# Four accumulators with sums in place, fewer late chunks, and the residual's bias moved within DRAM, in a two-layer backbone on TensorE

## The chip, the cores and the metric

The kernel runs on one core of one Trainium2 chip. The metric is device time in microseconds (us) of one execution. The engines are TensorE (PE in the profile, with its weight loads as PEld), VectorE (DVE), ScalarE (ACT), GpSimd (POOL) and SyncE (SP). Data lies in DRAM, in the on-chip SBUF (128 partitions) and in PSUM, where TensorE's sums appear. In this kernel SP issues the loads of weights, and POOL issues the stores and all transfers that add to what lies in DRAM.

## The reference

512 latent and 256 context tokens of width 1024 pass through two layers. Each layer is a half-step gated feed-forward network (FFN), a mixer, and another FFN; the mixer is a gated MLP over chunks of tokens (gMLP) in the first layer and attention in the second. Each of these six sub-layers is modulated by a shift, a scale and a gate, and ends in a layer norm over a scaled residual. What matters here is cut from it:

```python
def modulation(cond, w_mod, b_mod):
    m = jax.nn.silu(cond) @ w_mod + b_mod          # 9 vectors of 1024 for each layer and condition
    return jnp.split(m[..., None, :], N_MOD, axis=-1)

def ffn_sublayer(x, shift, scale, gate, w_in, w_out, ln_g, ln_b):
    y = swiglu(modulate(x, shift, scale), w_in, w_out)
    return layer_norm(ALPHA * x + 0.5 * gate * y, ln_g, ln_b)

# gMLP: x <- layer_norm(ALPHA * x + gate * gmlp_mix(h)); attention likewise
```

There are two conditions: one for the latent tokens and one for the context tokens. The last four of the 18 modulation vectors are needed for the latent tokens alone. All is 32-bit.

## The kernel before, in words

**Products.** Every 32-bit operand is split into a high and a low part, and each product is three matmuls. The weights come in slices of 128x512: SP loads a `raw` (six places), ACT casts the high part into a unit `w`, DVE subtracts to get the low part. There are `W_BUFS` such units. In the first three FFNs the input products of a tile are done by Strassen's scheme: a tile is seven products of 12 matmuls with sums of weights (`sums`) and of inputs (`comb`), and DVE adds up the results (`pieces`, `q`).

**Sub-layers.** They are numbered n = 0 to 5: FFN, gMLP, FFN, FFN, attention, and an FFN over the latent tokens alone. By the profile they occupy about 97 to 640 us (n = 0), 640 to 1256 (n = 1), 1360 to 1814 (n = 2), 1930 to 2383 (n = 3), 2383 to 2600 (n = 4), and 2600 to the end (n = 5). The stretches between are the layer norms with the openings of the next sub-layer. Each FFN has 22 tiles of 128 hidden columns in six chunks (`FFN_CHUNKS`), and gMLP has 24 in six chunks of four. After each chunk comes a projection `out_proj`: two halves of the width by six blocks of tokens (four at n = 5), a sum over the chunk's tiles in one bank of PSUM for each. All but the last chunk's sums leave by one of two ways, in the helper `accumulate`:

- **late** chunks, the first `LATE_CHUNKS` = 4: ACT copies the sum to a `q` (lines 669 or 75) and POOL adds it to `ysum` in DRAM (line 437). When the gate is known, `late_unit` reads `ysum` back, DVE multiplies it by the gate into an `acc`, and POOL adds that to `zsum` in DRAM.
- later chunks: DVE multiplies the sum by the gate into a `q` (line 658 or 75), and POOL adds it to `zsum` (line 443).

**Work in between.** `fill` takes the next step of a row of generators, between the products of tiles and banks:

- `residual_unit`: loads the gain and the bias of the layer norm before into two `acc` tiles, reads each half of a block of normalised tokens (`zhat`) into an `mraw`, multiplies and adds on DVE (line 411 or 75), and lets POOL write it to `zsum`.
- `mod_unit`: one of the 18 vectors of modulation. Eight `mraw` slices of `w_mod` for each half are scaled and summed on DVE into one `acc` for each condition (lines 354 and 356), POOL adds up the 128 partitions (`partition_all_reduce`, line 362) into a `row`, and a transfer adds the row to `mod` in DRAM (line 363).
- `late_unit`, as above.

There are two `acc` tiles, two `row` tiles and three `mraw` tiles. In gMLP one `row` is taken for the whole sub-layer by `kept`, where the sums `w_sR` of the spatial weights lie. In the three Strassen FFNs the six first tiles are opened during the layer norm, and the pieces of the sixth lie in the two `row` tiles until it is finished.

**Order.** Each engine works through its instructions in order. In the Strassen FFNs the order on DVE and ACT is fixed as the program issues it (`pin`), with a product's reading of PSUM two products behind (`slot`); elsewhere a scheduler places them. `Lnnn` in a row is the line; in pinned stretches all operations have line 75.

Of the kernel before, what the change touches and what calls it, by code (L numbers as in the profile page):

```python
# [13 lines left out]
P = 128  # L14
D = 1024
# [23 lines left out]
FFN_CHUNKS = [4, 4, 2, 4, 4, 4]  # L39
GMLP_CHUNKS = [4, 4, 4, 4, 4, 4]  # L40
W_BUFS = 10
RAW_BUFS = 6
MRAW_BUFS = 3

LATE_CHUNKS = 4
# [11 lines left out]
    [(0, 5), (0, 6), (0, 7), (0, 8), (1, 0)],  # L57
    [(1, 1), (1, 2), (1, 3)],
    [(1, 4), (1, 5), (1, 6), (1, 7)],
# [20 lines left out]
class Backbone:  # L80
# [254 lines left out]
    def acc(self):  # L335
        return self.main.tile([P, 512], F32, tag="acc", bufs=2, name="acc")

    def mod_unit(self, l, i):
# [7 lines left out]
        for half in range(2):  # L346
            accs = [self.acc() for _ in range(nconds)]
            for k0 in range(0, KD, per):
# [9 lines left out]
                yield  # L358
            s = slice(half * 512, half * 512 + 512)
            for c in range(nconds):  # L360
                out = self.main.tile([P, 512], F32, tag="row", bufs=2, name="row")
                nc.gpsimd.partition_all_reduce(out, accs[c], P, bass_isa.ReduceOp.add)  # L362
# [3 lines left out]
        if i % 3 == 1:  # L366
            self.later(READ_LATER, lambda: self.mod_columns(l, i - 1))
        elif i % 3 == 2:
            self.mod_done.add((l, i))

# [26 lines left out]
    def residual_unit(self, prev, nblocks):  # L397

        for half in range(2):
            s = slice(half * 512, half * 512 + 512)  # L400
            rows = []
            for name in ("ln_g", "ln_b"):
                row = self.acc()
                self.sp.dma_start(row, self.io[name][prev[0], prev[1], s].unsqueeze(0).to_broadcast([P, 512]))
                rows.append(row)
            self.filler_raw()
            yield
            for b in range(nblocks):
                raw = self.next_raw()
                for row, op in zip(rows, (ALU.mult, ALU.add)):  # L410
                    self.dve.tensor_tensor(raw, raw, row, op)
                self.add_to_z(b, half, raw)
                self.filler_raw()
                yield
# [30 lines left out]
    def begin_sublayer(self, n, l, i, nblocks, prev):  # L445
# [14 lines left out]
        if n == 0:  # L460
            units += [mods.pop(0), self.vectors_rest(), self.copies()]
        else:
# [4 lines left out]
        if (l, i) != (1, 3):  # L467
            units.append(self.late_unit(nblocks))
        self.filler = (s for u in units for s in u)

    def copies(self):

        for b in range(NB):
# [4 lines left out]
            yield  # L478
# [211 lines left out]
    def out_proj(self, acts, factor, nblocks, end=None, late=False):  # L690
# [54 lines left out]
    def new_pieces(self, f):  # L745
# [9 lines left out]
        elif f == 5:  # L755
            self.pieces += [self.main.tile([P, 512], F32, tag="row", bufs=2, name="pieces")[:, 0:HT] for _ in range(2)]
# [62 lines left out]
    def ffn(self, l, i, nblocks, end):  # L819
        if self.hooks:  # L820
            self.opening()
        self.pin(True)
        for ci, size in enumerate(FFN_CHUNKS):
            last = ci == len(FFN_CHUNKS) - 1
            acts = []
            if ci == LATE_CHUNKS:
# [8 lines left out]
            self.out_proj(acts, 0.5, nblocks, end if last else None, ci < LATE_CHUNKS)  # L835
# [51 lines left out]
    def ffn_latent(self, l, i, nblocks, end):  # L887
        tiles = self.tiles_latent()
        for ci, size in enumerate(FFN_CHUNKS):
            last = ci == len(FFN_CHUNKS) - 1  # L890
            acts = []
            if ci == LATE_CHUNKS:
# [12 lines left out]
            self.out_proj(acts, 0.5, nblocks, end if last else None, ci < LATE_CHUNKS)  # L905


    def token_proj(self, blocks, evacuate, fills=1, between=None):
# [19 lines left out]
        for group in groups:  # L928
            for b in group:
                banks[b] = self.bank()  # L930
            for k in range(KD):
                w = ws[k] if len(groups) > 1 else self.weights(1)[0]
                for b in group:
                    part(w, k, b)
                    if k == KD - 1:
                        evacuate(b, banks[b])
                if group is groups[-1]:
# [7 lines left out]
    def gmlp(self, l, i, nblocks, end):  # L945
# [5 lines left out]
        kept = self.main.tile([P, 4, P], F32, tag="row", bufs=2, name="w_sR")  # L951
# [18 lines left out]
        for cc in range(CC):  # L970

            def evacuate(b, ps):
                v = self.q(512)
                act.activation(v, ps, AF.Gelu)
                dve.bn_stats(vst[b][:, cc], v)
                nc.gpsimd.dma_start(spill[cc][b * P : b * P + P, :], v)

            if cc == CC - 1:
                following = group(0)
                next(following)  # L980
            self.token_proj(range(NB), evacuate)
        next(following)
        grp = next(following)
        vbox = self.box("v", F32)[:, :].rearrange("p (n b t) -> p n b t", n=4, b=NB)
# [4 lines left out]
        def fetch(j):  # L989
            if j < GMLP_CH:  # L990
                vr = vbox[:, j % 4]
# [51 lines left out]
        for ci, n in enumerate(GMLP_CHUNKS):  # L1043
            acts = []
            if ci == LATE_CHUNKS:
                self.load_gate(l, i + 2, nblocks)
                self.start_late(nblocks)
            for j, m in zip(range(j0, j0 + n), self.acts_places(n, TOK)):
# [42 lines left out]
                self.fill(int(j + 1 < GMLP_CH))  # L1091
            j0 += n
            self.out_proj(acts, 1.0, NB, end if j0 == GMLP_CH else None, ci < LATE_CHUNKS)
# [51 lines left out]
    def attention(self, l, i, nblocks, end):  # L1145
# [12 lines left out]
        self.load_gate(l, i + 2, NB_LAT)  # L1158
        self.rope_t = self.gate[:, 1, 0:512].rearrange("p (b s f) -> p b s f", b=NB_LAT, s=2)
# [133 lines left out]
        ws = [self.main.tile([P, 2, 4, P], F32, tag="w", bufs=W_BUFS, name="q_tok") for _ in range(2)]  # L1293
        self.wlive += 2
        q_tok.append([ws[b // 2][:, b % 2] for b in range(NB_LAT)])
# [10 lines left out]
        out_at = {14: (0,), 16: (1,), 18: (2, 3)}  # L1306
# [7 lines left out]
        for n in range(len(units)):  # L1314
# [14 lines left out]
            if n < 14 and n >= 4 and n % 3 == 1:  # L1329
                q_transposed(1, n // 3 - 1)  # L1330
                if n == 13:
                    self.release(2)
# [186 lines left out]
    def body(self):  # L1519
        self.weight_order()  # L1520
        self.mseq, self.mraw, self.pending, self.hooks, self.begun, self.pieces = [], [], [], [], [], []
        self.mod_done, self.mods, self.zhat = set(), {}, None
# [20 lines left out]
class End:  # L1543
# [5 lines left out]
    def begin(self, nblocks):  # L1549
# [3 lines left out]
        while k.pending:  # L1553
            k.fill()
# [127 lines left out]
```

## Time and profile before

| what | value |
|---|---|
| time before, median of 3 runs | 3075.28 us (3073.64 to 3080.31) |
| the profiled execution's own time | 3070.61 us |
| its span | 3068.8 us |
| mean granted TensorE clock in it | 0.969 |
| PE busy | 2834.6 us, 92% |
| DVE busy | 2124.6 us, 69% |
| ACT busy | 1261.2 us, 41% |
| POOL busy | 664.8 us, 22% |

Busy shares are averages over the whole span. In timelines a row is a run of like instructions: start, duration, engine, line, operation, `out<-in`, tile shapes, count, and in brackets the idle time ahead of it with what ended it. In tables of waits a row is engine, what it wanted to do, what it waited for, and then total us, times, and the longest. A row of stretches lists its ends and length, the busy time and instructions of each engine, the granted clock, and the load of the 16 DMA engines.

### The profile page before, as it was taken

The page shows a single profiled execution, that of the slowest core. Times are in us where ns is not written, and L with a number is a line of the kernel's source. Part 1 is how long each engine was busy: PE and PEld are TensorE (multiplying, and loading weights), DVE is VectorE, ACT ScalarE, POOL GpSimd, SP SyncE. Part 2 cuts the span into 40 slices and gives each one's busy share as a digit, 9 for nine tenths or more (in the row PEclk, how much of TensorE's full clock was granted, in tenths as well). Part 3 has the DMA queues.
Part 4 walks back from the last instruction along what each step waited for, and adds up shares of the span by engine and source line. Part 5 has one row for each costly group of instructions (what it writes and reads, how often), then busy time and mean ns, then how long its engine had stood idle before and what let it go on. Part 6 is the DMA issues. An engine that isn't in the chain of part 4 may idle for free. (4 is left out here: it accounts for less than half of the span.)

```text
span 3068.8 us, 41397 instructions
## 1 busy us (share of the span) xinstructions
PE 2834.6 (92%) x14454; PEld 2539.3 (83%) x14454; DVE 2124.6 (69%) x3726; ACT 1261.2 (41%) x2425; POOL 664.8 (22%) x682
## 2 busy tenths in 40 slices
PE   5899999998989899998999898898998979989998
PEld 4898998887878798888898798788888868878886
DVE  5985886766576545897788679777676758763345
ACT  5444342522444453553343246333333536633332
POOL 1022222113234212101323300132211121120121
PEclk9999999999999899999999999999999989999999
DMA  8446657466366667545666744666676431375583
GB/s 264 119 150 140 154 148 169 172 226 208 114 189 152 137 143 153 158 138 196 158 157 147 169 137 142 212 143 174 156 170 141 140 95 41 104 240 134 127 190 112
DMA packets 428891, 476.98 MB, mean 155 GB/s; under 512 B 30697, under 2 KB 282793, under 8 KB 428585
## 3 DMA queue, kind: packets, MB, share of 16 engines
q1 hardware_dynamic: 368056, 340.90, 36.2%
q0 software_dynamic: 60624, 133.43, 21.2%
q8 instruction: 113, 1.85, 0.2%
q14 instruction: 98, 0.79, 0.1%
HBM read 345.13 MB, written 132.35 MB: 156 GB/s over the span
## 5 line engine op out<-in xcount | busy, mean ns | idle before, releaser
L75 PE MATMUL ps<-comb,w 128*128 128x384 f32 x5544 | 999.2, 340 | 94.8 <-DVE q L75 47.1
L75 PEld LDWEIGHTS ps<-comb,w 128*128 128x128 f32 x5544 | 980.2, 191 | 109.2 <-DVE q L75 51.1
L75 PE MATMUL ps<-w,acts 128*128 128x512 f32 x3768 | 877.3, 393 | 23.7 <-ACT acts L75 12.7
L75 PEld LDWEIGHTS ps<-w,acts 128*128 128x128 f32 x3768 | 709.1, 189 | 178.4 <-ACT acts L75 15.8
L75 PE MATMUL ps<-h,w 128*128 128x384 f32 (+2 forms) x2304 | 451.5, 356 | 1.7 <-DVE w L142 0.9
L75 PEld LDWEIGHTS ps<-h,w 128*128 128x128 f32 x2304 | 407.7, 190 | 39.8 <-PE ps L75 1.3
L142 DVE TENSOR_TENSOR w<-raw,w 128x512 fp32r<-128x512 f32 x391 | 271.3, 705 | 213.6 <-ACT w L141 212.0
L141 ACT CAST w<-raw 128x512 fp32r<-128x512 f32 x391 | 238.8, 621 | 394.5 <-PE ps L75 277.6
L362 POOL PARTITION_ALL_REDUCE row<-acc x56 | 202.8, 3625 | 567.7 <-DVE acc L75 367.2
L437 POOL DMA_DIRECT2D ysum<-q x224 | 188.9, 974 | 625.5 <-ACT q L75 338.8
L75 PE MATMUL ps<-w,h 128*128 128x512 f32 x1200 | 283.4, 398 | 21.0 <-DVE kT L136 9.7
L75 PEld LDWEIGHTS ps<-w,h 128*128 128x128 f32 x1200 | 230.2, 193 | 71.9 <-DVE kT L136 10.3
L75 DVE TENSOR_TENSOR w<-raw,w 128x512 fp32r<-128x512 f32 x353 | 263.2, 748 | 26.9 <-ACT w L75 26.9
L75 ACT CAST w<-raw 128x512 fp32r<-128x512 f32 x353 | 216.5, 619 | 125.3 <-PE ps L75 72.1
L75 DVE SCALAR_TENSOR_TENSOR acc<-mraw,cs,acc 128x512 f32<-128x512 f32 x238 | 169.6, 745 | 54.5 <-DMA mraw<-in_w_mod_dram 54.1
L75 ACT CAST w<-sums 128x512 fp32r<-128x512 f32 x180 | 111.6, 620 | 198.7 <-DVE sums L280 105.0
L75 ACT COPY q<-ps 128x512 f32<-128x512 f32 (+1 forms) x193 | 106.9, 558 | 200.7 <-PE ps L75 144.7
L75 DVE TENSOR_TENSOR q<-q,ps 128x384 f32<-128x384 f32 x274 | 150.2, 548 | 54.8 <-PE ps L75 53.0
L75 DVE TENSOR_TENSOR w<-sums,w 128x512 fp32r<-128x512 f32 x180 | 130.0, 722 | 38.0 <-ACT w L75 37.4
L75 ACT CAST acts<-q 128x384 fp32r<-128x384 f32 x104 | 53.5, 514 | 242.1 <-DVE q L75 242.1
L163 POOL TENSOR_TENSOR rs<-ve,mhalf 128x1 f32<-128x1 f32 (+3 forms) x47 | 40.7, 866 | 478.6 <-DVE ve L160 337.4
L354 DVE SCALAR_TENSOR_TENSOR acc<-mraw,cs,acc 128x512 f32<-128x512 f32 x154 | 113.4, 773 | 35.2 <-DMA mraw<-in_w_mod_dram 34.4
(189 smaller groups left out, 2593.8 us busy)
## 6 DMA issues: line engine op xcount, KB each, us to landing
raw<-in_ffn_w_in_dram SPq DMA_DIRECT2D x386, 256.0 KB
mraw<-in_w_mod_dram SPq DMA_DIRECT2D x256, 256.0 KB
ysum<-q POOLq DMA_DIRECT2D x224, 256.0 KB, 5.2
raw<-in_ffn_w_out_dram SPq DMA_DIRECT2D x176, 256.0 KB
raw<-in_gmlp_w_in_dram SPq DMA_DIRECT2D x96, 256.0 KB
zsum<-q POOLq DMA_DIRECT2D x64, 256.0 KB, 6.1
z<-zsum SPq DMA_DIRECT2D x32, 512.0 KB
mraw<-ysum SPq DMA_DIRECT2D x56, 256.0 KB
```

Of the source, the lines that this page charges most:

```text
L75: return self.tc.keep_in_program_order(f(*args, **kwargs))
L141: self.act.copy(hi, src)
L142: self.lows.append((key, lambda: self.dve.tensor_tensor(lo, src, hi.bitcast(F32), ALU.subtract)))
L163: self.last_rstd = self.nc.gpsimd.tensor_tensor(rs, ve, self.mhalf[:, 0:1].to_broadcast([P, n]), ALU.pow).ins
L354: dve.scalar_tensor_tensor(accs[c], raw, cs, accs[c], ALU.mult, ALU.add)
L362: nc.gpsimd.partition_all_reduce(out, accs[c], P, bass_isa.ReduceOp.add)
L437: self.nc.gpsimd.dma_start(self.ysum[b][:, half * 512 : half * 512 + 512], src, accum_op=op)
```

## The change

- FFN chunks are 4, 3, 3, 4, 4, 4 tiles; one weight unit is given up (9), `mraw` has five places, `acc` four, and the `row` tag is gone.
- POOL's sum over partitions writes over its own `acc`. The pieces of the sixth opened tile lie in two `acc` tiles. `w_sR` lies in a fourth of gMLP's `v` box, which leaves three slots for `v`.
- The late chunks are 2, 1, 1 and 2 for n = 0, 2, 3 and 5, and none in gMLP. With that 64 sums leave PSUM by ACT and `ysum` where 224 did, and 224 by DVE and `zsum` where 64 did; `late_unit` has 44 steps where it had 56.
- The residual's bias is written to `zsum` from `ln_b` by POOL, DRAM to DRAM, 512 KB for each block. DVE only multiplies by the gain, into an `acc` of its own, which POOL then adds to `zsum`. The gain is loaded anew every three blocks.
- Fewer fills: a mod vector takes 16 steps where it took 20 (8 where 12), a Strassen tile has one or two fills in turn, and the tiles that were opened have one. The last mod vector of n = 5 comes ahead of its residual. `MOD_PLAN` moves (1,1) to gMLP, and (1,5) to n = 2.
- In attention the second half of `q` lies in the gate's place and the gate is loaded later.

**DVE, first projection of the second FFN of layer 0** (n = 2), up to the first Strassen tile behind it. `acc<-mraw,cs` are steps of a mod vector, `mraw<-mraw,acc` and `acc<-mraw,acc` the residual's products, `q<-q,ps` the tile's first additions. Before:

```order
L293 TENSOR_TENSOR sums<-raw,sums 128x512
L75 TENSOR_TENSOR mraw<-mraw,acc 128x512 x2
L75 TENSOR_SCALAR acc<-mraw,cs 128x512 x2
L75 SCALAR_TENSOR_TENSOR acc<-mraw,cs,acc 128x512 x4
L75 TENSOR_TENSOR w<-raw,w 128x512
L75 TENSOR_TENSOR q<-q,ps 128x384
L75 TENSOR_TENSOR w<-sums,w 128x512
L75 TENSOR_TENSOR w<-raw,w 128x512
L279 TENSOR_TENSOR sums<-raw 128x512
L75 TENSOR_TENSOR q<-q,ps 128x384
```

The same place in the changed kernel; six more products `acc<-mraw,acc` stand ahead of the first row:

```order
L75 TENSOR_TENSOR acc<-mraw,acc 128x512
L75 TENSOR_TENSOR w<-sums,w 128x512
L280 TENSOR_TENSOR sums<-sums,raw 128x512
L75 TENSOR_TENSOR acc<-mraw,acc 128x512 x2
L75 TENSOR_TENSOR w<-sums,w 128x512
L293 TENSOR_TENSOR sums<-raw,sums 128x512
L75 TENSOR_TENSOR q<-q,ps 128x384
L75 TENSOR_TENSOR w<-raw,w 128x512
L75 TENSOR_TENSOR w<-sums,w 128x512
L75 TENSOR_TENSOR acc<-mraw,acc 128x512
L75 TENSOR_TENSOR q<-q,ps 128x384
```

Before, all 24 operations of the residual and the first steps of a mod vector stand ahead of the first `q<-q,ps`. Now nine of the residual's twelve products stand ahead of it and the tenth ahead of the second one, and no step of a mod vector. All ten products write to the same place in SBUF: of the four `acc` tiles two hold pieces and one the gain. At n = 3 the ten stand in the same way.

**DVE in gMLP, between the third projection and the fourth** (`L354`, `L356`: mod vectors; `L142`: low parts of weights; `L966`, `L967`: `w_sR`). Before:

```order
L356 TENSOR_SCALAR acc<-mraw,cs 128x512
L354 SCALAR_TENSOR_TENSOR acc<-mraw,cs,acc 128x512 x12
L142 TENSOR_TENSOR w<-raw,w 128x512 x3
L966 COPY w_sR<-ps 128x128
L1075 SCALAR_TENSOR_TENSOR su<-ps,sguT,s_8888 128x256
L142 TENSOR_TENSOR w<-raw,w 128x512
L967 TENSOR_TENSOR w_sR<-w_sR,ps 128x128
```

In the changed kernel (`L667`: a sum that leaves PSUM with the gate; `L982`, `L983`: `w_sR` in the `v` box):

```order
L667 SCALAR_TENSOR_TENSOR q<-ps,gate 128x512
L354 SCALAR_TENSOR_TENSOR acc<-mraw,cs,acc 128x512 x3
L667 SCALAR_TENSOR_TENSOR q<-ps,gate 128x512
L354 SCALAR_TENSOR_TENSOR acc<-mraw,cs,acc 128x512
L142 TENSOR_TENSOR w<-raw,w 128x512 x2
L667 SCALAR_TENSOR_TENSOR q<-ps,gate 128x512
L142 TENSOR_TENSOR w<-raw,w 128x512 x2
L982 COPY v<-ps 128x128
L1090 SCALAR_TENSOR_TENSOR su<-ps,sguT,s_8895 128x256
L983 TENSOR_TENSOR v<-v,ps 128x128
```

The runs of 12 steps of a mod vector are now broken by gated sums every three steps.

The diff, cut:

```diff
-FFN_CHUNKS = [4, 4, 2, 4, 4, 4]
+FFN_CHUNKS = [4, 3, 3, 4, 4, 4]
-W_BUFS = 10
+W_BUFS = 9
-MRAW_BUFS = 3
+MRAW_BUFS = 5
-LATE_CHUNKS = 4
+LATE_CHUNKS = {(0, 0): 2, (0, 6): 1, (1, 0): 1, (1, 6): 2}
...
     def acc(self):
-        return self.main.tile([P, 512], F32, tag="acc", bufs=2, name="acc")
+        return self.main.tile([P, 512], F32, tag="acc", bufs=4, name="acc")
...
             for c in range(nconds):
-                out = self.main.tile([P, 512], F32, tag="row", bufs=2, name="row")
-                nc.gpsimd.partition_all_reduce(out, accs[c], P, bass_isa.ReduceOp.add)
-                nc.gpsimd.dma_start(m[c : c + 1, s], out[0:1, :], accum_op=ALU.add)
+                nc.gpsimd.partition_all_reduce(accs[c], accs[c], P, bass_isa.ReduceOp.add)
+                nc.gpsimd.dma_start(m[c : c + 1, s], accs[c][0:1, :], accum_op=ALU.add)
             yield
-            yield
...
     def residual_unit(self, prev, nblocks):
 
+        bias = self.io["ln_b"][prev[0], prev[1]].unsqueeze(0).to_broadcast([P, D])
+        for b in range(nblocks):
+            self.nc.gpsimd.dma_start(self.zsum[b], bias)
+            self.z_begun |= {(b, 0), (b, 1)}
+            if b % 2:
+                yield
         for half in range(2):
-            s = slice(half * 512, half * 512 + 512)
-            rows = []
-            for name in ("ln_g", "ln_b"):
-                row = self.acc()
-                self.sp.dma_start(row, self.io[name][prev[0], prev[1], s].unsqueeze(0).to_broadcast([P, 512]))
-                rows.append(row)
-            self.filler_raw()
-            yield
             for b in range(nblocks):
-                raw = self.next_raw()
-                for row, op in zip(rows, (ALU.mult, ALU.add)):
-                    self.dve.tensor_tensor(raw, raw, row, op)
-                self.add_to_z(b, half, raw)
+                if b % 3 == 0:
+                    gain = self.acc()
+                    s = slice(half * 512, half * 512 + 512)
+                    src = self.io["ln_g"][prev[0], prev[1], s]
+                    self.sp.dma_start(gain, src.unsqueeze(0).to_broadcast([P, 512]))
+                    yield
+                raw, out = self.next_raw(), self.acc()
+                self.dve.tensor_tensor(out, raw, gain, ALU.mult)
+                self.add_to_z(b, half, out)
                 self.filler_raw()
                 yield
...
-                    self.accumulate(b, half, acts, ws, factor, int(n > 2 or b % 2 == 0), late)
+                    self.accumulate(b, half, acts, ws, factor, int(dense or b % HALF < 2), late)
...
         elif f == 5:
-            self.pieces += [self.main.tile([P, 512], F32, tag="row", bufs=2, name="pieces")[:, 0:HT] for _ in range(2)]
+            self.pieces += [self.acc()[:, 0:HT] for _ in range(2)]
...
-                fills = 0 if last and f == size - 1 else 2
+                fills = 0 if last and f == size - 1 else 1 + f % 2
...
-            self.out_proj(acts, 0.5, nblocks, end if last else None, ci < LATE_CHUNKS)
+            self.out_proj(acts, 0.5, nblocks, end if last else None, ci < late, ci < late or ci == 4)
...
-        kept = self.main.tile([P, 4, P], F32, tag="row", bufs=2, name="w_sR")
+        vbox = self.box("v", F32)
+        kept = vbox[:, 3 * TOK : 3 * TOK + 4 * P].rearrange("p (n t) -> p n t", n=4)
+        vbox = vbox[:, 0 : 3 * TOK].rearrange("p (n b t) -> p n b t", n=3, b=NB)
```

More of the change, by code (lines that the diff above doesn't have):

```diff
@@ L822, in ffn @@
         self.pin(True)
+        late = LATE_CHUNKS[l, i]
         for ci, size in enumerate(FFN_CHUNKS):
@@ L1292, in attention @@
         self.psum_layout(PAIRS)
-        ws = [self.main.tile([P, 2, 4, P], F32, tag="w", bufs=W_BUFS, name="q_tok") for _ in range(2)]
-        self.wlive += 2
-        q_tok.append([ws[b // 2][:, b % 2] for b in range(NB_LAT)])
+        q1 = self.main.tile([P, NB_LAT, 4, P], F32, tag="gate", bufs=1, name="q_tok")
+        q_tok.append([q1[:, b] for b in range(NB_LAT)])
         for x in range(N_KV):
```

68 lines of the change are left out of this document (38 added, 30 removed).

## The prediction

> **What bounds the kernel now.** I read the page's first two parts, then TensorE's waits, then its timeline at each long wait with DVE's timeline ahead of it.
>
> ```profile
> PE 2834.6 (92%) x14454; PEld 2539.3 (83%) x14454; DVE 2124.6 (69%) x3726; ACT 1261.2 (41%) x2425; POOL 664.8 (22%) x682
> ```
>
> TensorE is the bound, and the change leaves its matmuls alone. What can be won is its idle time, 3068.8 − 2834.6 = 234 us at most, and the half clock that follows a long wait. So I went through TensorE's waits by stage; gMLP first (640 to 1256 us, the waits of PE):
>
> ```profile
> PE ps L75 <- DVE w_sR L967: 17.9, 2, 17.7
> PE ps L75 <- DVE w_sT L136: 17.6, 3, 11.6
> PE ps L75 <- ACT q L974: 8.5, 1, 8.5
> ```
>
> ```profile
> 740.41 67.07 PE L75 MATMUL ps<-w,h 128*128 128x512 f32 x282 [8.50 <-ACT q L974]
> ...
> 914.28 0.58 PE L75 MATMUL ps<-w_sT,ones 128*128 128x256 f32 x1 [11.58 <-DVE w_sT L136]
> ...
> 1009.76 1.19 PE L75 MATMUL ps<-w_sT,vn 128*128 128x256 f32 x4 [17.75 <-DVE w_sR L967]
> 1010.94 10.96 PE L75 MATMUL ps<-h,w 128*128 128x384 f32 x48
> ...
> 1023.26 8.49 PE L75 MATMUL ps<-h,w 128*128 128x384 f32 x48
> ```
>
> 44.0 us of waits here. The last two rows show what follows one: the same 48 matmuls take 10.96 us behind the wait and 8.49 later, so 2.5 us more is lost at the lower clock. Before the 17.75 us DVE did this:
>
> ```profile
> 991.04 0.49 DVE L356 TENSOR_SCALAR acc<-mraw,cs 128x512 f32<-128x512 f32 x1 [4.66 <-POOL row L362]
> 991.57 1.54 DVE L354 SCALAR_TENSOR_TENSOR acc<-mraw,cs,acc 128x512 f32<-128x512 f32 x2
> ...
> 997.72 1.41 DVE L354 SCALAR_TENSOR_TENSOR acc<-mraw,cs,acc 128x512 f32<-128x512 f32 x2 [2.07 <-DMA mraw<-in_w_mod_dram]
> ...
> 1002.23 2.74 DVE L354 SCALAR_TENSOR_TENSOR acc<-mraw,cs,acc 128x512 f32<-128x512 f32 x4 [1.19 <-DMA mraw<-in_w_mod_dram]
> 1004.88 1.88 DVE L142 TENSOR_TENSOR w<-raw,w 128x512 fp32r<-128x512 f32 x3
> ```
>
> DVE is not full; it stands in a queue of mod steps. The next half waits for POOL to free an `acc`, the loads then restart from three empty `mraw` places, and the spatial weights that TensorE wants are behind all that. Over the run, and for the late units:
>
> ```profile
> DVE acc L75 <- DMA mraw<-in_w_mod_dram: 56.8, 22, 11.7
> DVE acc L356 <- POOL row L362: 46.1, 15, 5.3
> DVE acc L658 <- DMA mraw<-ysum: 44.9, 4, 13.1
> DVE acc L658 <- DMA zsum<-acc: 23.2, 7, 6.4
> ```
>
> The FFNs' waits, out of several answers of the timeline:
>
> ```profile
> 506.88 5.30 PE L75 MATMUL ps<-comb,w 128*128 128x384 f32 x17 [6.06 <-ACT q L75]
> 1754.68 2.37 PE L75 MATMUL ps<-comb,w 128*128 128x384 f32 x12 [2.89 <-ACT q L75]
> 1758.83 3.06 PE L75 MATMUL ps<-comb,w 128*128 128x384 f32 x12 [1.79 <-DVE q L75]
> 1766.69 8.59 PE L75 MATMUL ps<-comb,w 128*128 128x384 f32 x38 [4.79 <-DVE q L75]
> 2737.26 8.06 PE L75 MATMUL ps<-w,acts 128*128 128x512 f32 x21 [8.41 <-ACT acts L135]
> ```
>
> The first four follow `late_unit` steps that wait for transfers on `ysum` and `zsum`; the last follows mod steps. At n = 3 (1930 to 2383) both kinds stand together:
>
> ```profile
> PE ps L75 <- DVE q L75: 27.5, 6, 9.2
> PE ps L75 <- ACT q L75: 7.1, 2, 4.3
> ```
>
> **The change part by part**, as gains (+) and losses (−) against the profiled 3070.6 us.
>
> gMLP: four `acc` tiles in place let the next half begin while POOL still sums the last, five `mraw` places keep two more loads ahead, the late unit is gone, and the mod steps come in threes. The waits (44.0) and three half clocks (7.5) make 51.5 us. Between, 48 more sums leave by DVE. I take 85%: **+44**; bounds 22 (the rows at 991 to 1002 show that loads hold the steps about as much as POOL does) and 51.
>
> Sums by DVE instead of ACT, all over the kernel:
>
> ```profile
> L658 DVE SCALAR_TENSOR_TENSOR q<-ps,gate 128x512 f32<-128x512 f32 x84 | 57.4, 685 | 35.9 <-PE ps L75 35.7
> L669 ACT COPY q<-ps 128x512 f32<-128x512 f32 x80 | 46.7, 587 | 117.9 <-PE ps L75 92.3 <-DMA ysum<-q 17.9 <-issue 6.6
> L411 DVE TENSOR_TENSOR mraw<-mraw,acc 128x512 f32<-128x512 f32 x56 | 37.6, 688 | 27.3 <-DMA mraw<-zhat 14.3 <-DMA acc<-in_ln_g_dram 3.6 <-issue 3.4
> ```
>
> 160 × 0.685 = 110 us more for DVE, 160 × 0.587 = 94 less for ACT; 52 residual additions × 0.688 = 36 and 12 late steps × 0.69 = 8 less for DVE. DVE goes to 2124.6 + 110 − 36 − 8 = 2191, or 71% of the span. TensorE covers it, since the gated sums that DVE reads already have cost it nothing: it waits for DVE `q` at the tiles, not at the projections.
>
> ```profile
> 1360.00:1814.00 454.00, 428.88 (x2215) 398.57 (x2215) 345.36 (x562) 163.02 (x304) 117.18 (x107) 0.97 0.64 162
> ```
>
> In the FFNs at n = 2 DVE has 345 of 454 us, and 36 × 0.685 − 12 × 0.688 = 16 more makes 80%. Without that cover a sum waits behind whatever DVE does; I put **−8** for it and for POOL's sums over partitions holding DVE as before (0 to −16).
>
> Late units: n = 0, half the chunks and reading earlier: 6.06 + 2.5 of clock, +8. n = 2: 9.47 + 1.5, four fifths: +9. n = 3: 27.5 + 7.1 less the 9.2 at the opening is 25.4, with three half clocks (6.5) 31.9; its mod vectors for one condition eat two loads a step, and five places help only in part, so three quarters: +24. n = 5: 8.41 + 2.5, just over half, since the mod vector only moves: +6. Together **+47**; half that, and all of it (62), are the bounds.
>
> The residual in series is the part against it. At the opening of n = 2 and 3 ten products go through one `acc` place, so each waits until the transfer of the one before has landed, and behind the tenth is the `q<-q,ps` that TensorE's fourth product of the tile needs. Before:
>
> ```profile
> 1376.27 0.55 DVE L75 TENSOR_TENSOR q<-pieces,ps 128x384 f32<-128x384 f32 x1
> ...
> 1377.80 0.69 DVE L75 TENSOR_TENSOR w<-raw,w 128x512 fp32r<-128x512 f32 x1
> ```
>
> ```profile
> 1377.76 32.84 PE L75 MATMUL ps<-w,acts 128*128 128x512 f32 x144
> 1410.44 6.43 PE L75 MATMUL ps<-comb,w 128*128 128x384 f32 x36
> 1425.40 12.38 PE L75 MATMUL ps<-comb,w 128*128 128x384 f32 x60 [8.53 <-DVE q L75]
> ```
>
> ```profile
> 1977.96 12.57 PE L75 MATMUL ps<-comb,w 128*128 128x384 f32 x60 [9.21 <-DVE q L75]
> ```
>
> ```profile
> ysum<-q POOLq DMA_DIRECT2D x224, 256.0 KB, 5.2
> zsum<-q POOLq DMA_DIRECT2D x64, 256.0 KB, 6.1
> zsum<-acc POOLq DMA_DIRECT2D x56, 256.0 KB, 5.7
> zsum<-mraw POOLq DMA_DIRECT2D x52, 256.0 KB, 3.4
> ...
> zsum<-in_x_dram POOLq DMA_DIRECT2D x4, 512.0 KB, 7.1
> ```
>
> Let T be 1377.76, the projection's start. In the new order the first product stands behind that `w<-raw,w`, so at about T + 0.6. A period P is one product, 0.69, and one landing. The tenth starts nine periods later; with its own 0.69 and the 0.55 of `q<-q,ps` TensorE goes on at T + 9P + 1.8. It is ready at 1410.44 + 6.43 = T + 39.1. The wait is 9P − 37.3. No row is of this transfer: `zsum<-mraw` is near in place but only writes, the others add as the new one does. I take `ysum<-q`, 5.2, whose load is the same stretch's: P = 5.9, wait 15.8, that is 7.3 and 6.6 more than the 8.53 and 9.21 now, with some half clock 8 each: **−16**. Ends: landing 3.4, P = 4.1, no wait, +18; landing 7.1 (`zsum<-in_x_dram`), P = 7.8, wait 32.9, −48.
>
> The Trainium skill (DMA: Bandwidth & Descriptors, "Anatomy of one DMA — SWDGE (gpsimd) path") fits a GpSimd transfer as 2.0 us and its bytes over 436 GB/s, which for 256 KB gives an estimate of 2.6 us and thereby no wait at all. The trace's adding transfers take twice that, the plain one 3.4, so I don't sum by it; it is rival B's case.
>
> Attention loses 8 residual additions ahead of its prelude, 5.5 us of DVE, where PE waits often: **+3** (0 to 6). A weight unit fewer: the transitions ask for eight units at once for the last projection, and one instead of two is then in hand, **−3** (0 to −8). The bias, 26 transfers of 512 KB on POOL, lies beside POOL's idle 78%; if one held up the queue it would be by its landing, some 7 us, in the chain above.
>
> Sum: 44 + 47 + 3 − 16 − 8 − 3 = **67**. The profiled execution comes to 3003.6; the median shown is 4.7 above the profiled execution's time, so I say **3008**.
>
> **The rivals.**
>
> A. The forecast: waits behind mod and late steps go, a residual wait of some 16 us comes at n = 2 and 3.
>
> B. Faster still: landings near 3.4 us, so the chain hides under the 39.1 us. For it: `zsum<-mraw`, at the same place; against: all three adding rows. The −16 becomes +18, and 5 of half clock: 67 + 34 + 5 = 106, or **2969**.
>
> C. It does not do what it says: loads, not places, hold the mod steps, and half of the gains remain. For it the 56.8 us on `mraw` against 46.1 on `row`; against, that two more places and three-step runs are for just that. 22 + 23 + 3 − 16 − 8 − 3 = 21, or **3054**.
>
> D. Slower: the chain decides. The gains without it are 83; each of the two waits would have to grow by 41.5 to 50.4, so P = 9.7 and landings of 9.0 us. At 10 us P = 10.7, each wait is 59 and costs 50: 83 − 100 = −17, or **3092**. For it: SP loads the gain anew within the chain, three times, and with an adding transfer, its 512 KB bias ahead and `ysum` all queued on POOL, 9 is not far; against: the rows' 5.2 to 6.1.
>
> **How the numbers follow.** A 0.63 (2980 to 3035), B 0.14, C 0.14, D 0.09. The range is **2966 to 3058**: B to C with the bounds of the chain between. A median tells apart about 0.2%, 6 us. A, B and most of C are faster: **0.86**; D slower, **0.09**; same **0.05**.
>
> **What would show it.** Right: no wait of PE over 5 us between 900 and 1020, `acc<-mraw` waiting for POOL under 15 us in all, DVE near 71%, two PE waits of 10 to 20 us at the first Strassen tile behind the first projection at n = 2 and 3, their DVE waiting for `zsum<-acc`. Wrong: these two above 40 us or below 5, new waits of PE for DVE `q` at the projections, or gMLP's waits still there under `mraw`.

## The result, and the profile after

| | before | after |
|---|---|---|
| median of 8 runs each | 3074.88 us | 3058.48 us (3052.41 to 3069.84) |
| profiled execution | 3070.61 us | 3069.84 us |

The changed kernel is faster: ratio 0.9948, 95% interval 0.9932 to 0.9965, so 16.4 us of the 67 that were forecast. Its profiled execution is the slowest of its eight; nothing below rests on a difference of a few us between the two traces as a whole.

First the page of the changed kernel, and TensorE's waits in its gMLP (640 to 1256 us; engine, what it waited for, total, times, longest):

```profile
PE 2831.2 (92%) x14454; PEld 2539.5 (83%) x14454; DVE 2211.2 (72%) x3822; ACT 1179.2 (38%) x2265; POOL 683.8 (22%) x696
```

```profile
PE ps L75 <- DVE w_sT L136: 6.8, 3, 3.7
PE ps L75 <- DVE q L667: 5.2, 3, 2.9
PE ps L75 <- DVE vn L136: 3.2, 1, 3.2
PE ps L75 <- DVE su L1090: 2.7, 4, 1.6
PE ps L75 <- ACT acts L135: 1.6, 2, 1.1
```

DVE is at 72%, as summed. The waits of 11.58 and 17.75 us in gMLP are gone; 19.5 us of waits are left in all, where the kernel before had 46.1 (44.0 in its three largest rows). DVE's waits for POOL's sums over partitions, 55.1 us before, are gone too. What came in their place shows in TensorE's timeline, out of four answers:

```profile
1358.36 11.08 PE L75 MATMUL ps<-w,acts 128*128 128x512 f32 x48
...
1391.44 6.43 PE L75 MATMUL ps<-comb,w 128*128 128x384 f32 x36
1420.57 3.75 PE L75 MATMUL ps<-comb,w 128*128 128x384 f32 x12 [22.70 <-DVE q L75]
```

```profile
1975.94 14.28 PE L75 MATMUL ps<-comb,w 128*128 128x384 f32 x70 [23.82 <-DVE q L75]
```

```profile
2477.14 3.35 PE L75 MATMUL ps<-w,h 128*128 128x512 f32 x7 [20.25 <-DVE kT L136]
```

```profile
2730.74 1.65 PE L75 MATMUL ps<-w,acts 128*128 128x512 f32 x3 [18.89 <-ACT acts L135]
```

Where 8.53, 9.21, 9.66 and 8.41 us stood before, there are 22.70, 23.82, 20.25 and 18.89 now: the openings of n = 2 and 3, attention, and the last FFN. DVE's waits over the run point to the cause. Before, the steps of line 75 waited 17.9 us for `zsum<-acc`, and the residual's products 16.7 us for the gain:

```profile
DVE acc L75 <- DMA zsum<-acc: 98.3, 23, 7.4
DVE acc L414 <- DMA acc<-in_ln_g_dram: 27.6, 5, 10.3
```

and DVE's timeline ahead of the first of them shows the chain at work, the first product and the last four:

```profile
1359.53 0.69 DVE L75 TENSOR_TENSOR acc<-mraw,acc 128x512 f32<-128x512 f32 x1
...
1400.45 0.69 DVE L75 TENSOR_TENSOR acc<-mraw,acc 128x512 f32<-128x512 f32 x1 [4.28 <-DMA zsum<-acc]
...
1405.67 0.69 DVE L75 TENSOR_TENSOR acc<-mraw,acc 128x512 f32<-128x512 f32 x1 [3.20 <-DMA zsum<-acc]
1411.26 0.69 DVE L75 TENSOR_TENSOR acc<-mraw,acc 128x512 f32<-128x512 f32 x1 [4.89 <-DMA zsum<-acc]
...
1419.27 0.69 DVE L75 TENSOR_TENSOR acc<-mraw,acc 128x512 f32<-128x512 f32 x1 [4.33 <-DMA zsum<-acc]
1419.88 0.55 DVE L75 TENSOR_TENSOR q<-q,ps 128x384 f32<-128x384 f32 x1
```

The tenth product starts 59.7 us after the first: nine periods of 6.64. The `q<-q,ps` right behind it ends at 1420.43, and TensorE goes on at 1420.57.

The two traces can be laid side by side, since TensorE issues the same 14454 matmuls. A row is the time from a given matmul, counted from the start, to another, in us:

| stretch | before | after | gained |
|---|---|---|---|
| n = 0 | 543.1 | 557.3 | −14.2 |
| gMLP | 615.9 | 585.0 | +30.9 |
| up to n = 2 and its first projection | 154.3 | 153.3 | +1.0 |
| first Strassen tiles behind it | 29.6 | 43.0 | −13.4 |
| rest of n = 2 | 374.1 | 363.9 | +10.2 |
| up to n = 3 and its first projection | 138.0 | 137.3 | +0.7 |
| first Strassen tiles behind it | 39.9 | 54.0 | −14.1 |
| rest of n = 3 | 391.1 | 368.8 | +22.3 |
| attention, to its scores | 217.0 | 216.5 | +0.5 |
| from there into the last FFN | 143.2 | 160.7 | −17.5 |
| rest | 311.9 | 316.8 | −4.9 |

The rows sum to a gain of 1.5 us only, because the changed kernel's trace lies 11.4 above its median and the other 4.3 below its own; so a row of a few us says little by itself.

### The profile page after: what moved, and what is told of

Read it like the earlier page. It is cut to its first block, busy times and chain, and to the rows that moved or that the text cites. A ratio compares the mean times of both kernels' runs of the same rounds, so it can differ in the third digit from the quotient of the medians.

```text
span 3068.1 us, 41411 instructions
## 1 busy us (share of the span) xinstructions
PE 2831.2 (92%) x14454; PEld 2539.5 (83%) x14454; DVE 2211.2 (72%) x3822; ACT 1179.2 (38%) x2265; POOL 683.8 (22%) x696
## 5 line engine op out<-in xcount | busy, mean ns | idle before, releaser
L142 DVE TENSOR_TENSOR w<-raw,w 128x512 fp32r<-128x512 f32 x354 | 246.2, 706 | 179.8 <-ACT w L141 176.3
L446 POOL DMA_DIRECT2D zsum<-q x224 | 209.9, 1056 | 628.5 <-DVE q L667 353.8
L75 DVE TENSOR_TENSOR w<-raw,w 128x512 fp32r<-128x512 f32 x390 | 279.8, 725 | 73.0 <-ACT w L75 73.0
L362 POOL PARTITION_ALL_REDUCE acc<-acc x56 | 199.6, 3572 | 393.2 <-DVE acc L75 264.1
L446 POOL DMA_DIRECT2D zsum<-acc x96 | 93.0, 1003 | 493.7 <-DVE acc L75 371.7
L75 DVE SCALAR_TENSOR_TENSOR acc<-mraw,cs,acc 128x512 f32<-128x512 f32 x266 | 190.0, 752 | 8.5 <-DMA mraw<-in_w_mod_dram 8.0
L75 DVE TENSOR_TENSOR w<-sums,w 128x512 fp32r<-128x512 f32 x183 | 146.4, 800 | 13.5 <-ACT w L75 13.1
L667 DVE SCALAR_TENSOR_TENSOR q<-ps,gate 128x512 f32<-128x512 f32 x148 | 101.2, 686 | 75.0 <-PE ps L75 74.8
```

The costliest lines, as they stand in the source:

```text
L75: return self.tc.keep_in_program_order(f(*args, **kwargs))
L142: self.lows.append((key, lambda: self.dve.tensor_tensor(lo, src, hi.bitcast(F32), ALU.subtract)))
L362: nc.gpsimd.partition_all_reduce(accs[c], accs[c], P, bass_isa.ReduceOp.add)
L446: self.nc.gpsimd.dma_start(self.zsum[b][:, s], src, accum_op=op)
L667: self.dve.scalar_tensor_tensor(tmp, ps, factor / ALPHA, self.gate[:, c, s], ALU.mult, ALU.mult)
```

## The experiments

Two theories stood after the result. **R**: the residual's products, which the change sends through `acc` and adds to `zsum` from there, make every product wait for a transfer. **S**: the 160 further sums that DVE reads and POOL adds to `zsum` cost what the places gained. All ratios are against the kernel before, run beside each of them on the same chip; its medians there lie between 3074.88 and 3082.44 us, so a difference of a few us between runs on different chips says less than their ratios.

**The product back in `mraw`.**

```diff
-                raw, out = self.next_raw(), self.acc()
-                self.dve.tensor_tensor(out, raw, gain, ALU.mult)
-                self.add_to_z(b, half, out)
+                raw = self.next_raw()
+                self.dve.tensor_tensor(raw, raw, gain, ALU.mult)
+                self.add_to_z(b, half, raw)
```

> One line of the change is taken back: the residual's product is written over its own mraw tile and added to zsum from there, instead of going through an acc tile. Bias, gain loads, late chunks and all else stay. Theory R (the products' way through acc ate the gain: the changed kernel's profile has waits of TensorE of 22.70 and 23.82 us at the openings of n = 2 and 3, 20.25 us in attention where 9.66 was, and 18.89 us in the last FFN where 8.41 was): the first two fall below 5 us, the other two go back to about 10 and 8, the sum is 22.7 + 23.8 - 8 + 10.6 + 10.5 = 60 with half clock on top: 2990 us (2975 to 3005). Rival S (the 160 further sums that DVE reads, and POOL's adding them to zsum, cost it): stays within 3045 to 3060.

3005.62 us, ratio 0.9769 (0.9754 to 0.9783): 53 us below the changed kernel, 55 by the ratios, by three lines. That is just past the end of theory R's range. TensorE in four answers of the timeline:

```profile
1402.26 8.04 PE L75 MATMUL ps<-comb,w 128*128 128x384 f32 x36 [3.09 <-DVE q L75]
```

```profile
1934.19 5.96 PE L75 MATMUL ps<-comb,w 128*128 128x384 f32 x24 [3.67 <-DVE q L75]
```

```profile
2419.67 5.61 PE L75 MATMUL ps<-w,h 128*128 128x512 f32 x16 [8.78 <-DVE kT L136]
```

```profile
2668.48 3.78 PE L75 MATMUL ps<-w,acts 128*128 128x512 f32 x8 [15.92 <-ACT acts L135]
```

The first three waits are 19.6, 20.2 and 11.5 us shorter, 51 of the 53 us; the fourth by 3.0 only, where theory R had said 10. Theory S falls. What R lacked is in the last FFN.

**Late chunks as before in the FFNs.**

```diff
-LATE_CHUNKS = {(0, 0): 2, (0, 6): 1, (1, 0): 1, (1, 6): 2}
+LATE_CHUNKS = {(0, 0): 4, (0, 6): 4, (1, 0): 4, (1, 6): 4}
```

> Four late chunks in the four FFNs, as before, so that 36 (24 in the last FFN's case fewer) sums in each go by ACT and ysum again; gMLP keeps none. Theory R, and the prediction's reading of the late units (reading ysum back late cost 6 us at n = 0, 9.5 at n = 2, about 17 at n = 3): 15 to 30 us slower than the changed kernel, about 3080. Rival S (sums by DVE and POOL's adding to zsum are what ate the gain): faster than the changed kernel by 10 us or more, below 3048, and the waits of 22.70 and 23.82 us at the openings shrink.

3063.11 us, ratio 0.9959 (0.9943 to 0.9975), which the changed kernel's interval overlaps. Neither theory's time came. TensorE's costliest waits are still those of the openings (22.8 and 23.9 us, within the first row), of the last FFN and of attention:

```profile
PE ps L75 <- DVE q L75: 68.1, 14, 23.9
PE ps L75 <- ACT acts L135: 20.7, 4, 18.7
PE ps L75 <- DVE kT L136: 20.5, 1, 20.5
```

The late waits of the kernel before, which I had put at 6 to 17 us a stage, did not come back with the chunks at the ends of n = 0, 2 and 3; only the wait at a mod vector of n = 3 grew, from 7.23 to 12.03 us. By the medians the number of late chunks in the FFNs is worth about 5 us in all. By the stretches of the two traces, a rough measure, four late chunks lose 3.1 us in the rest of n = 2 and 6.0 in that of n = 3, and gain 3.0 at n = 0 and 5.1 in the last row, where 311.7 us stand as in the kernel before.

**Five `mraw` places back to three, alone; and two tiles of their own for the sixth tile's pieces** (on top of that, for room).

```diff
-MRAW_BUFS = 5
+MRAW_BUFS = 3
```

> The changed kernel with three mraw places instead of five and nothing else. If four acc tiles in place are what freed gMLP (theory P, places for sums), gMLP's waits of TensorE, 44.0 us before and some 17 after, come back by less than 15 us and the time is within 0 to 20 us of the changed kernel. If the depth of the loads is what freed it (theory L), 25 to 35 us of waits return there, and the kernel is slower than the one before: 3080 to 3095 us.

3094.55 us, ratio 1.0065 (1.0042 to 1.0088): slower than before, which is theory L's time. Its waits are not quite L's: in gMLP they rise from 19.5 to 37.6 us, by 18, where L said 25 to 35 and P less than 15, and the stretch from 585.0 to 610.0. There TensorE now waits

```profile
PE ps L75 <- DVE q L667: 21.0, 9, 5.5
PE ps L75 <- DVE w_sT L136: 9.8, 2, 6.2
```

mainly for gated sums, and DVE's timeline shows them behind mod steps that wait for loads:

```profile
992.84 1.41 DVE L354 SCALAR_TENSOR_TENSOR acc<-mraw,cs,acc 128x512 f32<-128x512 f32 x2 [3.30 <-DMA mraw<-in_w_mod_dram]
994.88 0.75 DVE L354 SCALAR_TENSOR_TENSOR acc<-mraw,cs,acc 128x512 f32<-128x512 f32 x1 [0.62 <-DMA mraw<-in_w_mod_dram]
995.54 0.68 DVE L667 SCALAR_TENSOR_TENSOR q<-ps,gate 128x512 f32<-128x512 f32 x1
```

So the gated sums cost TensorE 5.2 us of waits in gMLP with five places and 21.0 with three.

```diff
-MRAW_BUFS = 5
+MRAW_BUFS = 3
...
-            self.pieces += [self.acc()[:, 0:HT] for _ in range(2)]
+            self.pieces += [self.main.tile([P, 512], F32, tag="six", bufs=2, name="pieces")[:, 0:HT] for _ in range(2)]
```

> The sixth opened tile's pieces lie in two tiles of their own, so that the residual at n = 2 and 3 has three acc tiles for its products; two mraw places are given up for the room (three instead of five). To be read against the run that gives up the two mraw places alone. Theory R: the waits of 22.70 and 23.82 us at the openings fall below 6 us, those in attention and the last FFN stay, so it is 35 to 45 us faster than that other run. Rival S: no more than 10 us between the two. A third reading, that loads hold the products (the mraw tiles wait for the same products), would leave the openings' waits above 15 us.

3067.37 us, ratio 0.9966 (0.9953 to 0.9979): 27 below the run with three places alone, against 35 to 45 expected. The openings' waits, 21.60 and 22.94 us with three places alone, are

```profile
1426.26 4.18 PE L75 MATMUL ps<-comb,w 128*128 128x384 f32 x12 [6.94 <-DVE q L75]
```

```profile
1960.33 4.18 PE L75 MATMUL ps<-comb,w 128*128 128x384 f32 x12 [4.75 <-DVE q L75]
```

and attention keeps 21.19. The first is a little above the 6 us expected, and both are below those of the kernel before (8.53 and 9.21): with three `acc` tiles for the products instead of one, what the chain had added is gone, even with three `mraw` places. The third reading (loads hold the products) falls.

**The whole residual as before** (gain and bias by DVE within `mraw`, written to `zsum`), all else as changed: `residual_unit` of the kernel before in the changed kernel.

```diff
-            self.nc.gpsimd.dma_start(self.zsum[b], bias)
...
+            for name in ("ln_g", "ln_b"):
+                row = self.acc()
...
+                raw = self.next_raw()
+                for row, op in zip(rows, (ALU.mult, ALU.add)):
+                    self.dve.tensor_tensor(raw, raw, row, op)
+                self.add_to_z(b, half, raw)
```

> The changed kernel with the whole residual as before: gain and bias loaded into two acc tiles, both applied by DVE within the mraw tile, then written (not added) to zsum. Against the run with the product within mraw (3005.6 us), this takes back the bias within DRAM as well: 52 DVE operations more (36 us), 26 transfers of 512 KB fewer, and plain writes (landing 3.4 us before) in place of adding ones (7.0 us in that run). Theory R1 (only the way through acc cost; the bias within DRAM is sound and saves DVE): 3005 to 3015. Theory R2 (adding is itself a price: it holds mraw places longer): 2990 to 3002, the last FFN's wait of 15.92 us goes back to about 8.

3008.85 us, ratio 0.9775 (0.9756 to 0.9794), not to be told from the run with the product within `mraw`. That is theory R1's time: these runs show no price and no gain of the bias within DRAM. The parts differ: attention waits 12.89 us (8.78), the last FFN 8.55 (15.92). The landing of what goes to `zsum` is 4.3 us here, written, and 7.0 there, added:

```profile
zsum<-mraw POOLq DMA_DIRECT2D x52, 256.0 KB, 4.3
```

```profile
zsum<-in_ln_b_dram POOLq DMA_DIRECT2D x26, 512.0 KB, 11.8
zsum<-mraw POOLq DMA_DIRECT2D x52, 256.0 KB, 7.0
```

**The last FFN.** First its order as before (the residual ahead of the mod vector), on top of the product within `mraw`:

```diff
-        elif n == 5:
-            self.mseq += srcs
-            units += mods
-            srcs = list(self.residual_srcs(nblocks))
-            mods = [self.residual_unit(prev, nblocks)]
```

> The product within mraw as in the run of 3005.6 us, and the last FFN's residual ahead of its mod vector, as before the change. That run has a wait of TensorE of 15.92 us there (8.41 before), ahead of which DVE waits 10.52 us for mraw<-zhat. If the order of the two units makes it: the wait falls to 8 to 10 and the time to 2995 to 3000. If it comes of five adding transfers at once, wherever they stand: the wait moves and stays above 13, 3003 to 3008.

3012.14 us, 0.9778 (0.9759 to 0.9798). The wait splits in two, 15.7 us together:

```profile
2659.80 2.01 PE L75 MATMUL ps<-w,acts 128*128 128x512 f32 x3 [9.19 <-ACT acts L135]
2668.35 1.22 PE L75 MATMUL ps<-w,acts 128*128 128x512 f32 x2 [6.54 <-ACT acts L135]
```

The order alone does not make it. Then that FFN's residual alone written as before, with the changed order and the product within `mraw` elsewhere:

```diff
-            mods = [self.residual_unit(prev, nblocks)]
+            mods = [self.residual_written(prev, nblocks)]   # residual_unit of the kernel before
```

> The product within mraw (3005.6 us), and in the last FFN alone the residual as before: bias by DVE, written and not added. There TensorE waits 15.92 us in the run with the product within mraw, 8.55 in the run with the whole residual as before. If five adding transfers at once (landings of 9 us there) hold the mraw places: the wait falls to about 8.5, and the time to 2995 to 3000. If it is the place of the mod vector ahead of it: no change, 3003 to 3008.

2999.38 us, ratio 0.9730 (0.9702 to 0.9759), the lowest time here, though the interval just meets that of the run with the product within `mraw`. The wait is as expected:

```profile
2655.82 4.34 PE L75 MATMUL ps<-w,acts 128*128 128x512 f32 x10 [8.45 <-ACT acts L135]
```

With the product within `mraw`, five adding transfers are issued there from 2648.70 to 2652.91 us and land 4.2, 7.1, 9.4, 9.2 and 9.6 us later. The three `zhat` loads that follow are issued just as the first three land (at 2652.89, 2656.38 and 2659.29). So the adding transfers hold the `mraw` places, and it is not the order that makes the wait. Written, the first five land in 2.7 to 7.0 us. But DVE's additions are back as well and space them out, over 7.2 us instead of 4.2; what each of the two is worth, no run tells apart. The time is 6 us lower by the medians and 12 by the ratios, the wait 7.5.

**One part of the change on the kernel before.** Four `acc` tiles with sums in place (and with them the pieces in `acc`, `w_sR` in the `v` box); and five `mraw` places with nine weight units:

> The kernel before with one part of the change: four acc tiles, POOL's sums in place, no row tiles, the pieces of the sixth tile in acc, w_sR in the v box. Three mraw places, ten weight units, late chunks and residual as before. Theory P (places for sums held gMLP): gMLP's waits of TensorE fall from 44 to about 20, 3045 us. Theory L (loads held it): gMLP keeps 35 us or more of waits, 3068 to 3078.

> The kernel before with the other part: five mraw places and nine weight units, all else as before. Theory L: gMLP's waits fall to about 20 and those at n = 3 (38.8 us) by half, 3040 us. Theory P: gMLP keeps 30 us or more; n = 3 gains 10, the weight unit costs 3: 3060 to 3070. If neither part alone frees gMLP, each waits for the other.

```diff
-        return self.main.tile([P, 512], F32, tag="acc", bufs=2, name="acc")
+        return self.main.tile([P, 512], F32, tag="acc", bufs=4, name="acc")
-                nc.gpsimd.partition_all_reduce(out, accs[c], P, bass_isa.ReduceOp.add)
+                nc.gpsimd.partition_all_reduce(accs[c], accs[c], P, bass_isa.ReduceOp.add)
```

and, for the other,

```diff
-W_BUFS = 10
+W_BUFS = 9
-MRAW_BUFS = 3
+MRAW_BUFS = 5
```

3046.39 us, 0.9896 (0.9881 to 0.9911), and 3043.05 us, 0.9886 (0.9866 to 0.9905). gMLP's waits, of the places alone and then of the loads alone:

```profile
PE ps L75 <- DVE w_sT L136: 15.4, 3, 11.2
PE ps L75 <- ACT q L975: 6.2, 1, 6.2
```

```profile
PE ps L75 <- DVE w_sT L136: 23.1, 3, 19.2
PE ps L75 <- ACT q L974: 6.2, 1, 6.2
```

In all, gMLP's waits are 27.0 and 36.9 us (46.1 before, 19.5 with all of the change), so each part frees some of it. The places' time is the one that theory P gave, the loads' time the one that theory L gave, though the waits that the loads leave are P's. The kernels are 33 and 36 us below the one before, the second with the lost weight unit in it. Their ratios multiplied give 0.978, and the changed kernel with the product within `mraw` is at 0.977. By stage the two do not agree, so that this is in part luck:

| stretch | before | changed | places alone | loads alone | changed, three `mraw` | changed, four late chunks |
|---|---|---|---|---|---|---|
| n = 0 | 543.1 | 557.3 | 547.9 | 559.2 | 558.8 | 554.3 |
| gMLP | 615.9 | 585.0 | 594.6 | 600.7 | 610.0 | 583.8 |
| rest of n = 2 | 374.1 | 363.9 | 364.8 | 371.1 | 361.0 | 367.0 |
| rest of n = 3 | 391.1 | 368.8 | 392.3 | 387.4 | 375.4 | 374.8 |

Of what the loads alone gain, 16 us lie at the openings of n = 2 and 3 (22.5 and 31.1 for the first Strassen tiles), which the changed kernel loses. The rest of n = 2 gains by the places. The 22.3 us in the rest of n = 3 come with neither part alone, and four late chunks or three `mraw` places lose only 6.0 and 6.6 of them. Late in that stretch TensorE waits 13.02 us with the places alone, and 4.41 and 6.13 us with the loads alone, while DVE waits for weights (14.24 and 8.49 us). The changed kernel has no such wait, not even with four late chunks. Whether both parts are needed, or it is another part of the change (one mod vector fewer at n = 3, mod vectors in 16 steps), no run tells.

**Nine weight units alone.**

```diff
-W_BUFS = 10
+W_BUFS = 9
```

> The kernel before with nine weight units instead of ten and nothing else. From the same matmul to the same matmul the first FFN (n = 0) takes 543.1 us in the kernel before, 557.3 in the changed one, 559.2 with five mraw places and nine units, 547.9 with the places for sums alone (ten units). Theory W (the tenth unit covers n = 0): it takes 553 us or more here, and the whole kernel 3086 to 3096. Theory V (five mraw places let loads of w_mod crowd out those of weights there): n = 0 stays within 543 to 548, and the kernel within 3075 to 3083, the predicted 3 us.

3090.40 us, ratio 1.0036 (1.0022 to 1.0050): the unit costs 11 us. It is lost at n = 0, 17.8 us longer in this trace though it has three `mraw` places; so theory V, by which five of them crowd out the weights, falls. The stretch of n = 0 (length, PE, PEld, DVE, ACT and POOL busy, clock, load, GB/s) in the kernel before, the changed one and this one:

```profile
97.00:640.00 543.00, 533.01 (x2762) 489.79 (x2762) 417.68 (x699) 219.78 (x413) 124.14 (x123) 0.99 0.59 155
```

```profile
95.60:653.00 557.40, 539.29 (x2763) 494.26 (x2763) 436.67 (x722) 210.11 (x392) 128.70 (x129) 0.98 0.60 158
```

```profile
98.00:658.80 560.80, 539.16 (x2762) 494.26 (x2761) 421.15 (x702) 222.27 (x416) 125.64 (x123) 0.98 0.57 150
```

**Two trims of the fastest kernel.** The gain loaded once for each half, and, apart from that, mod vector (1,6) in 16 steps of one load:

```diff
-                if b % 3 == 0:
+                if b == 0:
```

```diff
-        per = 3 - nconds
+        per = 1 if (l, i) == (1, 6) else 3 - nconds
```

> The same as e9_last with the gain loaded once for each half and not every three blocks: 10 loads of 256 KB fewer in SP's queue. If these loads cost anything once the products no longer wait for acc: 2 to 6 us faster than e9_last. If not: the same within 3 us.

3021.71 us, 0.9800 (0.9777 to 0.9822): 22 us slower. With two steps fewer for the residual every later step comes two fills earlier, and waits of 5.66, 6.70 and 6.61 us appear at n = 2 and 3. That the one makes the other is not shown.

> The same as e9_last with mod vector (1,6), the one of n = 3 that is for one condition and takes two loads of w_mod a step, in 16 steps of one load. TensorE waits 6.84 us there, with DVE waiting 6.23 us for a load of w_mod ahead of it. If two loads a step are what empties the five places: that wait falls below 3 us and the time by 4 to 8 us against e9_last. If the late unit at the end of n = 3 is then too late for its steps: a new wait of 5 us or more there, no gain.

3008.57 us, 0.9756 (0.9733 to 0.9779). The rival came, 9 us slower than without the trim: the old wait goes from 7.42 to 4.97 us, not below 3, and at the end of n = 3 there is a new one. It stands here with SP's and DVE's timelines ahead of it:

```profile
2279.77 3.47 PE L75 MATMUL ps<-comb,w 128*128 128x384 f32 x10 [14.15 <-DVE q L75]
```

```profile
2258.93 3.56 SPq L411 DMA_DIRECT2D acc<-in_ln_g_dram  x2
...
2270.63 0.33 SPq L411 DMA_DIRECT2D acc<-in_ln_g_dram  x1
2271.06 10.26 SPq L243 DMA_DIRECT2D raw<-in_ffn_w_in_dram  x5
```

```profile
2278.56 0.69 DVE L279 TENSOR_TENSOR sums<-raw 128x512 f32<-128x512 f32 x1 [15.27 <-DMA raw<-in_ffn_w_in_dram]
```

SP stands at loads into `acc` tiles, which the late unit's transfers still hold (17.2 us of its waits between 2255 and 2280 are for `zsum<-acc`), with the weights queued behind them.

## Why the prediction was wrong

The direction was right, and so were three places of the gain, gMLP, n = 2 and n = 3; the size was off by a factor of four, and the time lies 0.5 us beyond the range's end. What failed most is the price of sending the residual's products through `acc`: it was sized too small at n = 2 and 3 and left out in attention and the last FFN, and taking it back alone gave 53 us. Of the signs named, those of gMLP came. So did the two waits at n = 2 and 3, with DVE waiting for `zsum<-acc`, but above 20 us and not between 10 and 20. By the prediction's own steps:

- **"The residual in series" (−16)** was the right mechanism with too small a period. I took P = 5.9 and a wait of 15.8 us; it was 6.64 and 22.70 and 23.82. The arithmetic around it held: the first product at T + 1.2 (0.6 taken), TensorE ready at T + 39.5 (39.1). The period lacked POOL's way to the transfer. The ninth product starts at 1411.26 and its transfer is issued at 1412.25, 1.0 us later, not 0.69, and the tenth product starts 7.0 after that; on average 6.64 − 1.0 = 5.6 us are left for the landing, where I took 5.2. This landing, the slowest of the nine, took 7.0; the others took from 4.2 to 6.8:

```profile
1412.25 0.89 POOL L446 DMA_DIRECT2D zsum<-acc  x1 [3.61 <-DVE acc L75]
```

  Against the waits before, the two cost 14.2 and 14.6 us, not 7.3 and 6.6, and by the stretches 13.4 and 14.1.
- **"Attention +3"** and **"n = 5: +6"** missed that the same step works there. For attention I counted only the additions saved, for the last FFN only that the mod vector moves. Four `acc` tiles turn there, but the gain of the next three blocks needs one too. In attention its load is issued at 2459.97, when the transfer from an `acc` tile has landed (2459.95), and DVE waits for it:

```profile
2466.44 0.69 DVE L414 TENSOR_TENSOR acc<-mraw,acc 128x512 f32<-128x512 f32 x1 [5.77 <-DMA acc<-in_ln_g_dram]
```

  In the last FFN DVE waits 10.26 us for a gain whose load was issued at 2712.22, behind those of the gate and of `zhat`, and landed 9.8 us later. The gain before it had landed in 4.9, and the three products' adding transfers in between took 6.7 to 9.8:

```profile
2707.34 1.98 DVE L414 TENSOR_TENSOR acc<-mraw,acc 128x512 f32<-128x512 f32 x3 [4.23 <-DMA acc<-in_ln_g_dram]
...
2722.15 0.69 DVE L414 TENSOR_TENSOR acc<-mraw,acc 128x512 f32<-128x512 f32 x1 [10.26 <-DMA acc<-in_ln_g_dram]
```

  The waits of TensorE grew by 10.6 and 10.5 us where I had gains. In attention other waits made up for it in this trace (+0.5 by the stretch); up to the last FFN 17.5 us were lost, and 4.9 behind it, which the run with four late chunks does not lose.
- **"A weight unit fewer −3"** looked at the last projections. The unit costs 11 us of the whole, and it is lost at n = 0, where I had +8 and the trace has −14.2; no run shows the 3 us at the projections.
- **"gMLP +44"**: the waits fell by 26.6 and the stretch by 30.9; the share of 85% was too high. The lower bound of 22 rested on loads holding the steps about as much as POOL does. The two experiments with one part each bear that out: the places alone shorten the stretch by 21.3 us and the loads alone by 15.2.
- **"Late units +47"**: n = 2 and 3 gave 10.2 and 22.3 (9 and 24 said), but by the traces fewer late chunks were only some 3.1 and 6.0 of it, so that the sizes came right by luck. At n = 2 the places did the most; what did it at n = 3 stays open.
- **"Sums by DVE −8"**: DVE's share came as forecast, 72%. The price itself no run shows: with four late chunks, and so fewer of these sums, the kernel was 5 us slower. The bias, put at a landing of some 7 us, landed in 11.5 in the median; of the engines only POOL waits for it, 16 us in all.

By the stretches, forecast and trace lie 65.5 us apart: 28 in the last FFN, 22 at n = 0, 13 in gMLP, 12 in the two chains, 2 in attention and 1 at n = 2 and 3. From these go 13: the losses of 3 and 8, which I had put beside the stages, and 2 that the trace gained in the layer norms between. That trace lies 11 above the median. Rival C's time (3054) was near, for a reason that was mostly not C's: two thirds of the gain in gMLP and nearly all of it at n = 2 and 3 came, and D's mechanism, with landings between mine and D's, took most of it. B fell: the adding transfers landed in 5.4 to 6.5 us, not near 3.4.

```profile
zsum<-q POOLq DMA_DIRECT2D x224, 256.0 KB, 6.5
zsum<-acc POOLq DMA_DIRECT2D x96, 256.0 KB, 6.4
ysum<-q POOLq DMA_DIRECT2D x64, 256.0 KB, 5.4
```

The Trainium skill's fit for a GpSimd transfer (DMA: Bandwidth & Descriptors, "Anatomy of one DMA — SWDGE (gpsimd) path"), an estimate of 2.6 us for this size, does not hold for these adding transfers: they took twice that and more.

## What to carry to other kernels

When a change sends a result through a shared buffer on its way to a transfer, count at every place where it runs how many of these buffers are free, and price each turn as operation, issue and landing; a step that was right at two places stood unpriced at two others here. A load into such a buffer waits in SP's queue with all weights behind it. And price each buffer given up by a run of its own stage: the tenth weight unit looked idle at the projections and was worth 11 us of the whole kernel, lost in the first FFN.

## What the runs showed of the hardware

In this kernel an adding transfer of 256 KB to DRAM took 5.1 to 7.1 us from issue to landing, by the medians of each kind in each run, where a plain write from `mraw` took 3.4 to 4.3. In the last FFN of the run with the product within `mraw`, with five adding transfers issued within 4.2 us, DVE waited 10.5 us for a tile to come back and be loaded; with plain writes and DVE's additions between them TensorE's wait was 7.5 us shorter. The bias's 512 KB within DRAM took 11.0 to 12.6 us in the median, and those of `x` 6.8 to 8.3.
